# A hybrid S5 / short-conv / SwiGLU layer on one core: three pairs interleaved at the start, whole fp32 products for two block products, branch setup from step 0, smaller activation pieces, cosine product staged

## The chip, the core and the metric

One core of a Trainium2 chip runs the whole layer as one program. Its engines are TensorE (PE, matmul; PEld is its weight load), VectorE (DVE), ScalarE (ACT), GpSimd (POOL) and the DMA queues, nearly all issued from SyncE (SP). Each engine takes its instructions in the written order and waits on semaphores where an operand or a buffer is not ready. The metric is the device time of one execution in microseconds, the median over runs.

## The reference

```python
proj = jnp.einsum('bsd,dn->bsn', x, w_in) + b_in            # 1024 x 1024 -> 4096 columns
u, h, c_gate, b_gate, gate_a, gate_b = jnp.split(proj, [o1, o2, o3, o4, o5], axis=-1)
y_a = s5_ssm(u, ...)                                        # complex diagonal scan, 32 groups x 64 states
g = jax.nn.gelu(y_a)
y_a = g * jax.nn.sigmoid(jnp.einsum('bsc,ce->bse', g, glu_w) + glu_b)
y_a = jnp.einsum('bsc,cd->bsd', y_a, w_ssm_out)
z = causal_depthwise_conv(c_gate * h, conv_w)
y_b = jnp.einsum('bsc,cd->bsd', b_gate * z, w_conv_out)
merged = jax.nn.sigmoid(gate_a) * y_a + jax.nn.sigmoid(gate_b) * y_b
mix = jnp.einsum('bsd,de->bse', merged, w_o)
x = layer_norm(ALPHA * x + mix, ln1_g, ln1_b)
hid = jax.nn.silu(jnp.einsum('bsd,df->bsf', x, w_gate)) * jnp.einsum('bsd,df->bsf', x, w_up)
x = layer_norm(ALPHA * x + jnp.einsum('bsf,fd->bsd', hid, w_down), ln2_g, ln2_b)
```

Everything is float32; x is 1024 tokens by 1024 channels, the feed-forward width is 2816.

## The kernel before

**Products.** Every large matrix product is done at nearly float32 precision with three fast passes: an operand is split into a high part (`hi`, rounded to fp32r by ACT) and a low part (`lo`, the rest, by DVE), and `Entry.mm` (lines 178 to 182) adds lo·hi, hi·lo and hi·hi for each of four quarters of the contraction: 12 matmuls of 128x512. The input projection and the gate/up projection use a Strassen-like scheme over 2x2 blocks: a `Pair` is two weight tiles, and seven block products m = 1 to 7 replace eight (tables `WOP`, `XOP`). Products 3 and 4 take a plain weight block, 2 and 5 take a plain block of x and a sum of two weight blocks, 1, 6 and 7 take sums on both sides. So each of the seven x operands (`xh[m]`, `xl[m]`, 128 x 2048 elements) must be summed (m = 1, 3, 4, 6, 7) and split once at the start of a stage, and each weight operand once per product.

**One step per product.** `run` (line 310) writes the program: at step s it issues the weight sum for step s+4 (on POOL), the weight split for step s+3 (ACT and DVE), one piece of each background generator in `bg`, the 12 matmuls of step s, then the evacuations of what that product completed (`Pair.ev`). Stage A (the input projection) has 112 steps: pairs u0 and u2 interleaved, then hc0, hc1, gt0, b0, hc2, hc3, gt1, b2 and gt2 to gt7. u is the S5 input, hc and b the conv branch, gt the gates.

**Two forms of split.** `split` (line 120) writes hi to SBUF and subtracts with both operands in SBUF. `psplit` (line 131) lets ACT write hi twice, once to a PSUM staging bank `hp` and once to SBUF, and DVE subtracts with one operand in PSUM. psplit needs two staging banks, so then a pool has six matmul banks in place of eight.

**The start.** The x operands are made in halves of 1024 columns with `split` (`make_x`); of each sum one half is on DVE and one on POOL (`sum_x`), both hooked into steps 1 to 10.

**Background work.** `setup` (line 462) is some hundred short DVE instructions of 32 to 288 columns that make the S5 tables; it starts at step 12. Then `mats`, `rot` and `flow` make eight chunks of the scan: `flow` multiplies on PE into `psw`, ACT copies it to `w`, two DMAs swap its partition halves into `ws`, and DVE multiplies `psw` by the cosine table into `w`, in place over what the swap reads (line 719). psw lies in one of two PSUM slots (`sm`) that pst, pk, psw and psy of `mats` and `flow` share.

**Stage D.** The gate/up projection starts at step 168 with the pairs f0, f1, f2 interleaved over 21 steps. Its x operands (`make_x1`, line 1136) are made there in halves of 1024 columns with `split`; the PSUM pool has eight banks and no staging until step 189, so weight splits there are of the SBUF form too.

Of the kernel before, what the change touches and what calls it, by code (L numbers as in the profile page):

```python
# [47 lines left out]
def kernel(  # L48
# [121 lines left out]
    class Entry:  # L170
# [6 lines left out]

        def mm(self, ps, xh, xl, first, last):
            for k in range(4):
                PE.matmul(ps, self.lo[:, k, :], xh[:, k, :], start=first and k == 0, stop=False, skip_group_check=True)  # L180
                PE.matmul(ps, self.hi[:, k, :], xl[:, k, :], start=False, stop=False, skip_group_check=True)  # L181
                PE.matmul(ps, self.hi[:, k, :], xh[:, k, :], start=False, stop=last and k == 3, skip_group_check=True)  # L182

    class Pair:
        def __init__(self, s0, s1, nm, combos, epilogue):
# [3 lines left out]
            self.alt, self.z3, self.early, self.drops = False, None, False, {}  # L189
# [13 lines left out]
        def ev(self, m):  # L203
# [51 lines left out]
        def step(self, m):  # L255
# [19 lines left out]
            def do_mm():  # L275
# [4 lines left out]
                xh, xl = self.xc(m)  # L280
                en.mm(self.b[bi], xh, xl, first, True)
# [135 lines left out]
    def make_x(m, parts=1):  # L417
        op = XOP[m]
        h = xh[m] = xcp.tile([P, 4, 512], F32R, tag=f"xh{m}", name=f"xh{m}")
        l = xl[m] = xcp.tile([P, 4, 512], F32R, tag=f"xl{m}", name=f"xl{m}")  # L420
        if len(op) == 1:
            s = 4 // parts
            for q in range(parts):
                c = slice(s * q, s * q + s)
                split(h[:, c], l[:, c], xr[op[0]][:, c])
        else:
            for q in range(2):
                c = slice(2 * q, 2 * q + 2)
                split(h[:, c], l[:, c], xsum[m][q])

    xsum = {}

    def sum_x(m):
        op = XOP[m]
        a, b = xr[op[1]], xr[op[2]]
        xsum[m] = []
        for q in range(2):
            t = sp.tile([P, 2, 512], F32, tag="xsum", name=f"xs{m}_{q}", bufs=3)
            c = slice(2 * q, 2 * q + 2)
            tt(t, a[:, c], b[:, c], OPS[op[0]], G if q else V)  # L440
            xsum[m].append(t)

    pairs[1].alt = lambda nm: epi.tile([P, T], F32, tag="cv", name=nm, bufs=2)[:, 0:512]
    add_pairs(pairs, LEAD_A, 2)
# [16 lines left out]
    def setup():  # L461
        ramp = tb["ramp"] = stile([P, P], "ramp", "ramp")
        dss = tb["dss"] = stile([16, NG], "dss", "dss")
        mg = tb["mg"] = stile([P, 2], "mg", "mg")
        V.memset(mg[:, 0:1], MAGIC)
        V.memset(mg[:, 1:2], -MAGIC)
        nc.sync.dma_start(dss, dsk)
        nc.sync.dma_start(ramp, cst[:, P : 2 * P])
        nLre = tb["nLre"] = stile([P, NG, 9], "nLre", "nLre")
        Lim = tb["Lim"] = stile([P, NG, 9], "Lim", "Lim")  # L470
        Mre = tb["Mre"] = stile([P, NG, 8], "Mre", "Mre")
        sMim = tb["sMim"] = stile([P, NG, 8], "sMim", "sMim")
        E8 = tb["E8"] = stile([P, NG], "E8", "E8")
        ph8 = tb["ph8"] = stile([P, 2, NG], "ph8", "ph8")
        scr = [stile([P, 4 * P], t, f"scr_{t}") for t in ("w", "ws", "z", "zs")]
        used = [0] * 4

        def carve(*shape):
# [41 lines left out]
        th, hh, hl = carve(NG), carve(NG), carve(NG)  # L520
# [10 lines left out]
        V.scalar_tensor_tensor(pr[:, 3], hh, C3, pr[:, 3], ALU.mult, ALU.add)  # L531
        wrap(pr, tm)
# [6 lines left out]
        wrap(phh, th)  # L539
        add(phl, pr[:, 3], pr[:, 2])  # L540
# [1118 lines left out]
```

## Time and profile before

| | |
|---|---|
| median of three runs | 1295.02 us (1293.82 to 1295.74) |
| the profiled execution | 1294.12 us, span 1292.3 us |
| PE busy | 1207.6 us, 93% of the span |
| DVE busy | 860.5 us, 67% |
| POOL busy | 783.4 us, 61% |
| ACT busy | 737.0 us, 57% |
| DMA queue of SP | 38.2% of 16 engines, 123 GB/s to and from HBM |

The page gives PE's share over the whole span; what is left over, 85 us, is not spread evenly. Its line of 40 slices shows PE at 7 to 8 tenths in the first two slices (32 us each), at 9 nearly everywhere later, at 6 in the slice at 646 us, and at 7 to 6 in the last two. DVE and POOL show 8 or 9 tenths in just these early slices and around 646 us. So a reader looks at the start, at the stretch from 160 to 406 us with the scan's chunks, and at the start of stage D one by one.

### The profile page before, as it was taken

The numbers are of one execution on the slowest core, as the hardware profiler recorded it, in microseconds if no ns is written. First come the engines' busy times: TensorE is split into PE (matmuls) and PEld (weight loads), VectorE is DVE, ScalarE is ACT, GpSimd is POOL, SyncE is SP. The second block draws the span as 40 slices with busy tenths as digits, with TensorE's granted clock in tenths as the row PEclk, the third lists the DMA queues.
The fourth block names the chain that finished last, engine by engine and source line by source line (L and its number), as shares of the span: only waits on it lengthen the run. The fifth ranks groups of instructions, "written<-read, shape, count | busy, mean of one in ns | idle before, by whom it ended". The sixth has DMA issues, their size and how long they took to land. (4 is left out here: it accounts for less than half of the span.)

```text
span 1292.3 us, 16665 instructions
## 1 busy us (share of the span) xinstructions
PE 1207.6 (93%) x5365; PEld 981.3 (76%) x5365; DVE 860.5 (67%) x1319; ACT 737.0 (57%) x1288; POOL 783.4 (61%) x579
## 2 busy tenths in 40 slices
PE   7789899989899999999869999999999999999976
PEld 4577677777677888888757888888888887888756
DVE  6998688786676675688984444444344467667797
ACT  5645776778776252243433555555555555878841
POOL 4836878796862125123688777778778764544444
PEclk9989999999999999999989999999999999999988
DMA  5221343344446645224204423323222419845212
GB/s 198 74 94 46 103 117 97 116 153 144 141 140 223 204 139 199 79 98 147 98 33 145 165 82 114 106 91 122 107 98 98 155 66 348 296 135 171 70 54 77
DMA packets 88023, 166.07 MB, mean 129 GB/s; under 512 B 17792, under 2 KB 27008, under 8 KB 87680
## 3 DMA queue, kind: packets, MB, share of 16 engines
q1 hardware_dynamic: 87936, 165.00, 38.2%
q8 instruction: 43, 0.70, 0.2%
q14 instruction: 44, 0.36, 0.1%
HBM read 114.77 MB, written 44.83 MB: 123 GB/s over the span
## 5 line engine op out<-in xcount | busy, mean ns | idle before, releaser
L180 PE MATMUL ps_f<-x1h,wl_f 128*128 128x512 f32 x616 | 242.5, 394 | 13.1 <-DVE wl_f L115 9.5
L181 PE MATMUL ps_f<-x1l,wh_f 128*128 128x512 f32 x616 | 241.6, 392 | 2.8 <-DVE x1l L115 2.8
L182 PE MATMUL ps_f<-x1h,wh_f 128*128 128x512 f32 x616 | 241.3, 392 | 0.0
L115 DVE TENSOR_TENSOR wl_f<-t_f,hp 128x512 fp32r<-128x512 f32 x92 | 63.3, 688 | 166.0 <-ACT hp L137 166.0
L180 PEld LDWEIGHTS ps_f<-x1h,wl_f 128*128 128x128 f32 x616 | 116.7, 190 | 39.7 <-issue 8.5
L137 ACT ACTIVATE hp<-t_f 128x512 fp32r<-128x512 f32 x92 | 55.4, 602 | 148.7 <-POOL t_f L106 147.8
L181 PEld LDWEIGHTS ps_f<-x1l,wh_f 128*128 128x128 f32 x616 | 116.7, 189 | 27.7 <-DVE x1l L115 3.6
L182 PEld LDWEIGHTS ps_f<-x1h,wh_f 128*128 128x128 f32 x616 | 116.6, 189 | 24.3
L1481 PE MATMUL pe<-rBl,rAh 128*128 128x512 f32 x297 | 117.7, 396 | 8.8 <-DVE rBl L115 8.8
L106 POOL TENSOR_TENSOR tB<-B,B 128x512 f32<-128x512 f32 x55 | 71.3, 1296 | 83.1 <-DVE rBl L115 47.6
L1480 PE MATMUL pe<-rBh,rAl 128*128 128x512 f32 x297 | 117.6, 396 | 1.5 <-DVE acc L112 1.3
L1482 PE MATMUL pe<-rBh,rAh 128*128 128x512 f32 x297 | 116.9, 394 | 0.0
L180 PE MATMUL ps_gt<-xh,wl_gt 128*128 128x512 f32 x224 | 90.0, 402 | 5.4 <-ACT ea_gt L227 2.4
L182 PE MATMUL ps_gt<-xh,wh_gt 128*128 128x512 f32 x224 | 88.3, 394 | 0.0
L181 PE MATMUL ps_gt<-xl,wh_gt 128*128 128x512 f32 x224 | 87.7, 392 | 0.0
L106 POOL TENSOR_TENSOR t_f<-raw_f,raw_f 128x512 f32<-128x512 f32 x62 | 83.3, 1344 | 4.1 <-DVE wl_f L115 4.1
L1481 PEld LDWEIGHTS pe<-rBl,rAh 128*128 128x128 f32 x297 | 56.4, 190 | 23.8 <-DVE rBl L115 12.4
L1480 PEld LDWEIGHTS pe<-rBh,rAl 128*128 128x128 f32 x297 | 56.5, 190 | 14.9 <-DVE acc L112 2.1
L1482 PEld LDWEIGHTS pe<-rBh,rAh 128*128 128x128 f32 x297 | 56.5, 190 | 11.6
L106 POOL TENSOR_TENSOR t_f<-raw_f 128x512 f32<-128x512 f32 x43 | 57.2, 1340 | 10.2 <-DMA raw_f<-in_wgu 9.6
L109 POOL TENSOR_TENSOR hid<-sgf,ec_f 128x512 f32<-128x512 f32 x21 | 27.5, 1309 | 55.0 <-DVE sgf L109 31.8
L115 DVE TENSOR_TENSOR rAl<-As,hp 128x512 fp32r<-128x512 f32 x66 | 45.3, 687 | 20.7 <-ACT hp L137 14.9
(406 smaller groups left out, 3283.7 us busy)
## 6 DMA issues: line engine op xcount, KB each, us to landing
raw_f<-in_wgu SPq DMA_DIRECT2D x45, 512.0 KB, 3.9
As<-a_d SPq DMA_DIRECT2D x77, 256.0 KB, 3.5
a_d<-hs SPq DMA_DIRECT2D x55, 256.0 KB, 2.0
B<-in_wd SPq DMA_DIRECT2D x44, 256.0 KB, 5.3
raw_gt<-in_w SPq DMA_DIRECT2D x16, 512.0 KB, 4.5
s_d<-sg SPq DMA_DIRECT2D x32, 256.0 KB, 2.6
sgd<-s_d SPq DMA_DIRECT2D x16, 512.0 KB, 3.6
a_d<-hid SPq DMA_DIRECT2D x22, 256.0 KB, 2.2
```

The costliest lines, as they stand in the source:

```text
L106: eng.tensor_tensor(o, a, b, op)
L109: eng.tensor_tensor(o, a, b, ALU.mult)
L115: eng.tensor_tensor(o, a, b, ALU.subtract)
L137: S.activation(hp, raw, AF.Copy)
L180: PE.matmul(ps, self.lo[:, k, :], xh[:, k, :], start=first and k == 0, stop=False, skip_group_check=True)
L181: PE.matmul(ps, self.hi[:, k, :], xl[:, k, :], start=False, stop=False, skip_group_check=True)
L182: PE.matmul(ps, self.hi[:, k, :], xh[:, k, :], start=False, stop=last and k == 3, skip_group_check=True)
L1480: PE.matmul(ps, al[:, c], bh, start=kp == 0, stop=False)
L1481: PE.matmul(ps, ah[:, c], bl, start=False, stop=False)
L1482: PE.matmul(ps, ah[:, c], bh, start=False, stop=kp == NK - 1)
```

## The change

- The pair gt0 is drawn forward: u0, u2 and gt0 are interleaved over the first 21 steps, in the product order that stage D has (`LEAD`).
- For these three pairs, products 2 and 5 are done with four unsplit float32 matmuls (`mm_whole`) of the plain x quarter and the plain weight sum (`wsum`); x operands 2 and 5 are split last, for the pairs behind.
- `make_x` works in quarters of 512 columns, one per call, all sums on POOL, with `split` and `psplit` in turn, hooked behind the matmuls of steps 0 to 19.
- `setup` starts at step 0, cut into more pieces, with its tables in a pool of their own; five small loads go out on ACT's queue. The small PSUM pool opens at step 21, not 14.
- `flow` writes the cosine product at once into a staging tile `wc`; `z` has two buffers; the next chunk's scan waits for the rotation and not for `y`; `psy` comes one step later; `K` lies in a staging tile.
- Stage D has six banks and staging from its first step; `make_x1` works in quarters with `split` and `psplit` in turn; f2's first two banks are copied to SBUF (`kept`).

```diff
+        def mm_whole(self, ps, w, x, first, last):
+            for k in range(4):
+                PE.matmul(ps, w[:, k, :], x[:, k, :], start=first and k == 0, stop=last and k == 3, skip_group_check=True)
...
+            if self.kept:
+                for i, need in ((0, {2, 4}), (1, {5, 3})):
+                    if once(f"k{i}", need):
+                        kt = self.kept(i)
+                        S.activation(kt, self.b[i], AF.Copy)
+                        self.b[i] = kt
...
             def do_split(c=slice(0, 4)):
+                if m in self.whole:
+                    return
...
-                xh, xl = self.xc(m)
-                en.mm(self.b[bi], xh, xl, first, True)
+                if m in self.whole:
+                    en.mm_whole(self.b[bi], hold["t"], xr[XOP[m][0]], first, True)
+                else:
+                    en.mm(self.b[bi], *self.xc(m), first, True)
...
-    pairs = [mkpair(0, 1, "u0", epi_u, 0), mkpair(2, 3, "u2", epi_u, 2)]
     gp_ = [mkpair(16 + d, 24 + d, f"gt{d}", epi_g, d) for d in range(8)]
+    pairs = [mkpair(0, 1, "u0", epi_u, 0), mkpair(2, 3, "u2", epi_u, 2), gp_.pop(0)]
...
+    def make_x():
+        waiting = []
+
+        def low(h, l, k, src):
+            (psplit if k % 2 else split)(h[:, k], l[:, k], src)
+
+        for n, m in enumerate((4, 3, 1, 7, 6, 5, 2)):
+            op = XOP[m]
+            if len(op) == 3:
+                sums = xcp.tile([P, 4, 512], F32, tag=("xh2", "xl2")[n % 2], name=f"xs{m}")
+            h = xh[m] = xcp.tile([P, 4, 512], F32R, tag=f"xh{m}", name=f"xh{m}")
+            l = xl[m] = xcp.tile([P, 4, 512], F32R, tag=f"xl{m}", name=f"xl{m}")
+            for k in range(4):
+                if len(op) == 1:
+                    src = xr[op[0]][:, k]
+                else:
+                    src = sums[:, k]
+                    tt(src, xr[op[1]][:, k], xr[op[2]][:, k], OPS[op[0]], G)
+                waiting.append((h, l, k, src))
+                if len(waiting) > 2:
+                    low(*waiting.pop(0))
+                yield 1
...
+    for p in pairs[:3]:
+        p.drops = {4: 1}
+        p.whole = {2: wsum, 5: wsum}
+    add_pairs(pairs, LEAD, 3)
...
         ws = stile([P, 4, P], "ws", f"ws{cc}")
         swap(ws, w)
-        s["sin"] = True
+        c = slice(0, 127)
+        wc = stage(f"wc{cc}").rearrange("p (g k) -> p g k", g=4)
+        mul(wc[:, :, c], ps[:, :, c], s["C"])
         yield 2
-        c = slice(0, 127)
         mul(ws[:, :, c], ws[:, :, c], s["S"], G)
-        mul(w[:, :, c], ps[:, :, c], s["C"])
         yield 1
-        add(w[:, :, c], w[:, :, c], ws[:, :, c])
-        while cc and "y" not in st[cc - 1]:
+        add(w[:, :, c], wc[:, :, c], ws[:, :, c])
+        while cc and "rotated" not in st[cc - 1]:
             yield 1
-        z = stile([P, 4, P], "z", f"z{cc}")
+        z = stile([P, 4, P], "z", f"z{cc}", 2)
...
-        yield 3
+        s["rotated"] = True
+        yield 4
...
+        for q in range(4):
+            c = slice(128 * q, 128 * q + 128)
             if len(op) == 1:
                 src = blk(op[0])[:, q]
             else:
...
+                tt(src, blk(op[1])[:, q], blk(op[2])[:, q], OPS[op[0]], V if m == 7 and q % 2 else G)
+            yield lambda c=c, src=src, q=q: (psplit if q % 2 else split)(h[:, :, c], l[:, :, c], src)
...
+    fps[2].kept = lambda i: cst_["zp"].tile([P, 512], F32, tag=f"keep{i}", name=f"keep{i}")
...
     def begin_d0():
+        flush()
+        psum_open("psD", 6, True)
...
+    xg = make_x()
+    for n, cnt in enumerate((2, 2, 2, 1, 2, 1, 2, 1, 2, 1, 2, 1, 2, 2, 1, 2, 1, 1, 1, 1)):
+        steps[n].mid.append(lambda cnt=cnt: [next(xg, None) for _ in range(cnt)])
+    start(setup())
...
-    steps[12].pre.append(begin_ssm)
-    steps[14].pre.append(small_psum)
+    steps[21].pre.append(lambda: (flush(), small_psum()))
```

**DVE, first stage.** Before, around the split of x operands 1 and 4 (`xl` is a low part of x, `xs` a sum of x, `wl` a low part of a weight, `hp` a staging bank in PSUM):

```order
L115 TENSOR_TENSOR xl_212<-xs_1_186,xh_211 128x1024
L115 TENSOR_TENSOR wl_u_1_218<-t_u_1_188,hp_219 128x512
L106 TENSOR_TENSOR xs_0_239<-xr_109,xr_90 128x1024
L115 TENSOR_TENSOR wl_u_4_244<-raw_u_1_89,hp_245 128x512
L115 TENSOR_TENSOR xl_265<-xs_0_239,xh_264 128x1024
L115 TENSOR_TENSOR xl_265<-xs_1_241,xh_264 128x1024
L115 TENSOR_TENSOR wl_u_4_271<-raw_u_1_100,hp_272 128x512
```

After, around x operands 3 and 1 (`scr` is the scratch tile of `setup`):

```order
L115 TENSOR_TENSOR xl_208<-xs_206,hp_299 128x512
L115 TENSOR_TENSOR wl_u_3_307<-raw_u_0_110,hp_308 128x512
L545 SCALAR_TENSOR_TENSOR scr<-scr 128x32 x3
L118 TENSOR_SCALAR scr<-scr 128x32
L547 SCALAR_TENSOR_TENSOR scr<-scr 128x32
L115 TENSOR_TENSOR xl_273<-xs_271,xh_272 128x512
L115 TENSOR_TENSOR xl_273<-xs_271,hp_326 128x512
L106 TENSOR_TENSOR eb_u_330<-ps_u_0_149,ea_u_159 128x512
```

The sums of x have left DVE, the low parts are half as long and every second one reads PSUM, and the short instructions of `setup` stand between them.

**DVE, the second scan chunk of stage A.** Before, the cosine product stands close ahead of the sum that uses it:

```order
L109 TENSOR_TENSOR w_1351<-psw_1346,ctab_1087 128x4x127
L112 TENSOR_TENSOR eb_b_1296<-ps_b_2_1315,eb_b_1296 128x512
L115 TENSOR_TENSOR wl_hc_1_1427<-t_hc_1_1403,hp_1428 128x512
L112 TENSOR_TENSOR w_1351<-w_1351,ws_1353 128x4x127
L726 MEMSET zs_1441 128x4
```

After, it goes to a tile of its own (`wc`) and eight instructions lie between:

```order
L109 TENSOR_TENSOR wc_1203<-psw_1193,ctab_932 128x4x127
L112 TENSOR_TENSOR eb_hc_1070<-ps_hc_2_1099,eb_hc_1070 128x512
L115 TENSOR_TENSOR wl_gt_1_1222<-t_gt_1_1178,hp_1223 128x512
L115 TENSOR_TENSOR cp_1189<-cp_1189,ct_1190 128x576
L378 SCALAR_TENSOR_TENSOR zE_1245<-ps_hc_0_1016,b1s,hs_1146 128x512
L112 TENSOR_TENSOR ec_hc_1112<-ps_hc_3_1231,ec_hc_1112 128x512
L115 TENSOR_TENSOR wl_gt_4_1251<-raw_gt_1_1008,hp_1252 128x512
L378 SCALAR_TENSOR_TENSOR zE_1245<-ec_hc_1112,b1s,hs_1146 128x512
L115 TENSOR_TENSOR wl_gt_3_1278<-raw_gt_0_1032,hp_1279 128x512
L112 TENSOR_TENSOR w_1198<-wc_1203,ws_1200 128x4x127
```

The product is issued two steps earlier and no longer writes what the swap's DMAs read.

## Rows read from the trace of the kernel before

**Rows 1.** Stretches: length, busy (instructions) of PE, PEld, DVE, ACT, POOL, clock, DMA

```profile
12.60:60.90 48.30, 36.79 (x140) 26.21 (x139) 43.36 (x34) 32.09 (x49) 40.62 (x18) 1.00 0.32 108
160.00:200.00 40.00, 36.80 (x175) 30.01 (x176) 33.78 (x49) 26.62 (x48) 30.46 (x23) 0.92 0.38 114
200.00:406.00 206.00, 190.04 (x927) 155.18 (x925) 146.88 (x207) 158.31 (x266) 148.84 (x108) 1.00 0.46 140
627.00:676.20 49.20, 35.93 (x140) 27.56 (x139) 46.67 (x31) 19.49 (x29) 41.98 (x20) 0.92 0.13 50
```

**Rows 2.** Timeline of DVE and POOL, first 75 us: start, length, instruction

```profile
27.90 1.21 DVE L106 TENSOR_TENSOR xs<-xr,xr 128x1024 f32<-128x1024 f32 x1
...
30.24 2.38 POOL L106 TENSOR_TENSOR xs<-xr,xr 128x1024 f32<-128x1024 f32 x1
...
44.88 3.49 POOL L106 TENSOR_TENSOR xs<-xr,xr 128x1024 f32<-128x1024 f32 x1
...
46.02 0.68 DVE L115 TENSOR_TENSOR wl_u<-t_u,hp 128x512 fp32r<-128x512 f32 x1
...
57.36 1.28 POOL L106 TENSOR_TENSOR t_hc<-raw_hc 128x512 f32<-128x512 f32 x1
...
69.00 0.19 DVE L499 SCALAR_TENSOR_TENSOR scr_z<-scr_z 128x32 f32<-128x32 f32 x1
...
73.17 1.32 POOL L112 TENSOR_TENSOR ea_hc<-ea_hc,eb_hc 128x512 f32<-128x512 f32 x1 [7.52 <-ACT eb_hc L230]
...
73.37 1.17 DVE L501 TENSOR_SCALAR scr_zs<-scr_zs 128x32 f32<-128x32 f32 x1
```

**Rows 3.** Groups in 12.6 to 60.9 us: count, busy us, mean ns, idle before

```profile
L106 POOL TENSOR_TENSOR xs<-xr,xr 128x1024 f32<-128x1024 f32 x5 | 15.1, 3010 | 0.0
...
L115 DVE TENSOR_TENSOR xl<-xs,xh 128x1024 fp32r<-128x1024 f32 x10 | 21.3, 2134 | 2.7 <-ACT xh L121 2.5
L106 DVE TENSOR_TENSOR xs<-xr,xr 128x1024 f32<-128x1024 f32 x5 | 9.1, 1824 | 0.0
...
L115 DVE TENSOR_TENSOR xl<-xr,xh 128x1024 fp32r<-128x1024 f32 x2 | 3.5, 1770 | 0.8 <-ACT xh L121 0.8
```

**Rows 4.** Timeline of PE: first matmuls of products 15, 16 and 22

```profile
66.75 0.39 PE L180 MATMUL ps_hc<-xh,wl_hc 128*128 128x512 f32 x1
...
69.49 0.39 PE L180 MATMUL ps_hc<-xh,wl_hc 128*128 128x512 f32 x1
...
89.97 0.80 PE L180 MATMUL ps_hc<-xh,wl_hc 128*128 128x512 f32 x1 [3.83 <-DVE ec_hc L112]
```

**Rows 5.** Timeline of PE: unsplit float32 matmuls, two instructions to each

```profile
259.83 0.63 PE L642 MATMUL pst<-ident,bst 128*128 128x128 f32 x4 [2.09 <-ACT gy L768]
...
289.63 1.03 PE L648 MATMUL pk<-cp,bst 128*16 128x128 f32 x8 [1.48 <-DVE w L109]
```

**Rows 6.** PE's waits in 160 to 406 us, and the timeline around the longest

```profile
PE pk L648 <- DVE w L109: 11.9, 4, 5.5
PE psy L741 <- DVE z L115: 3.9, 3, 1.6
...
158.29 1.68 DVE L115 TENSOR_TENSOR cp<-cp,ct 128x576 f32<-128x576 f32 x1
...
163.20 1.86 PE L648 MATMUL pk<-cp,bst 128*16 128x128 f32 x8 [5.54 <-DVE w L109]
```

**Rows 7.** Groups of POOL and DVE in 627.0 to 676.2 us

```profile
L106 POOL TENSOR_TENSOR x1s<-M 128x1024 f32<-128x1024 f32 x6 | 19.2, 3207 | 4.7 <-DVE x1l L115 4.7
...
L115 DVE TENSOR_TENSOR wl_f<-t_f,wh_f 128x512 fp32r<-128x512 f32 x9 | 14.4, 1604 | 0.0
L115 DVE TENSOR_TENSOR x1l<-x1s,x1h 128x1024 fp32r<-128x1024 f32 x8 | 14.0, 1763 | 0.0
L115 DVE TENSOR_TENSOR x1l<-M,x1h 128x1024 fp32r<-128x1024 f32 x2 | 4.9, 2492 | 1.0 <-ACT x1h L121 1.0
L106 DVE TENSOR_TENSOR x1s<-M 128x1024 f32<-128x1024 f32 x2 | 4.5, 2292 | 0.0
```

More of the change, by code (lines that the diff above doesn't have):

```diff
@@ L262, in do_add @@
                 if len(op) == 3:
-                    if "t" not in hold:
+                    if "t" not in hold and m in self.whole:
+                        hold["t"] = self.whole[m]()
+                    elif "t" not in hold:
                         hold["t"] = wring.tile([P, 4, P], F32, tag="tmp", name=f"t_{self.nm}_{m}", bufs=2)
@@ L314, in run @@
             if s + 4 < len(steps) and steps[s + 4].add:
-                steps[s + 4].add(eng=V if steps[s + 4].addv else G)
+                steps[s + 4].add()
             if s + 3 < len(steps) and steps[s + 3].split:
@@ L431 @@
[L431 to L444, printed above, removed]
+    def make_x():
[18 more added lines that the diff above has]
+                yield 1
+        for w in waiting:
+            low(*w)
+            yield 1
@@ new lines, in load_f, with wsum @@
+    def load_f(p, i):
+        p.raw[i] = epi.tile([P, T], F32, tag="cv", name=f"xz{i}", bufs=2).rearrange("p (k q) -> p k q", k=KT)
+        nc.sync.dma_start(p.raw[i], p.src[i])
+    wsums = []
+    def wsum():
+        n = len(wsums)
+        if n in (0, 4):
+            wsums.append(xcp.tile([P, 4, 4, P], F32, tag=("xh5", "xl5")[n // 4], name=f"ws{n}"))
+        else:
+            wsums.append(wsums[n - 1])
+        return wsums[n][:, n % 4]
+    pairs[1].alt = stage
+    pairs[2].early = True
@@ L472, in setup, with carve @@
[L472 to L478, printed above, removed]
+        scr = xst.tile([P, 1216], F32, tag="scr", name="scr")
+        used = [96]
+        def carve(*shape, at=None):
             n = int(np.prod(shape))
-            i = min(i for i in range(4) if used[i] + n <= 4 * P)
-            t = scr[i][:, used[i] : used[i] + n]
-            used[i] += n
+            o = used[0] if at is None else at
+            if at is None:
+                used[0] += n
+            t = scr[:, o : o + n]
@@ L592, in setup @@
         ts(nLre, nLre, sgn[:, 0:1], -1.0, ALU.mult, ALU.mult)
+        while next(xg, None):
+            yield 1
+        close(xst_cm)
+        open_ssm()
         Tt = tb["T"] = []
@@ L1232, in x1_rest @@
     def x1_rest():
+        waiting = []
         for m in (3, 1, 7, 6):
[L1234 to L1239 removed]
+            for f in make_x1(m):
+                waiting.append(f)
+                if len(waiting) > 2:
+                    waiting.pop(0)()
+                yield
+        for f in waiting:
+            f()
+            yield
     x1g = x1_rest()
[L1241 removed]
+    for n, cnt in ((4, 2), (5, 2), (6, 2), (7, 2), (8, 1), (9, 2), (10, 1), (11, 2), (12, 2), (13, 2), (14, 1)):
         steps[n_d + n].mid.append(lambda cnt=cnt: [next(x1g, None) for _ in range(cnt)])
@@ L1324 @@
     nc.sync.dma_start(cws, convw)
-    x2h = xh[2] = xcp.tile([P, 4, 512], F32R, tag="xh2", name="xh2")
-    x2l = xl[2] = xcp.tile([P, 4, 512], F32R, tag="xl2", name="xl2")
     for q in range(2):
-        c = slice(2 * q, 2 * q + 2)
-        steps[0].add(c, V)
-        steps[0].split(c)
-        for k in (2 * q, 2 * q + 1):
-            split(x2h[:, k], x2l[:, k], x00[:, k])
+        steps[0].add(slice(2 * q, 2 * q + 2), V)
+    steps[0].split()
     steps[1].add(eng=V)
```

145 lines of the change are left out of this document (57 added, 88 removed).

## The prediction, written before the changed kernel was run

> **What bounds the kernel now.** I read the page first: PE is busy 93% of the span, so no other engine bounds the whole, and only PE's 85 us of idle time and a low clock can be given back. Then I asked stretch by stretch what PE waits for. A step at full pace takes 69.49 − 66.75 = 2.74 us, 12 matmuls of 0.2285 us [rows 4]; the seven products 15 to 21 keep that pace, and one wait of 3.83 us stands behind them, just before product 22 [rows 4].
>
> In the start, 12.6 to 60.9 us, PE is idle 48.3 − 36.8 = 11.5 us, and DVE (43.4) and POOL (40.6) are both nearly full, ACT (32.1) is not [rows 1]. The mean durations there are too long: a sum of x takes POOL 3.0 us and DVE 1.8, a low part of x takes DVE 2.1 [rows 3], while the shortest of the same shapes take 2.38 and 1.21 [rows 2]. One place shows why: a DVE instruction of 32 columns takes 0.19 us alone and 1.17 when it begins 0.2 us into a POOL instruction that ends at 74.49 [rows 2]. The two exclude each other when DVE has both operands in SBUF; low parts of weights, which read one operand in PSUM (`hp`), keep 0.68 even there (46.02, inside a POOL sum) [rows 2]. So I add POOL's work and DVE's SBUF-only work at their undisturbed lengths. In 12.6 to 60.9: POOL 13 x 1.28 + 5 x 2.38 = 28.5, DVE 17 x 1.21 = 20.6, in all 49.1 in 48.3 us, a ratio of 0.98. That sum, not PE, sets the start. In 627.0 to 676.2, where stage D makes its operands and PE is idle 13.3 us [rows 1], POOL has 6 x 2.38 + 12 x 1.28 = 29.6, DVE 12 x 1.21 + 13 x 0.68 = 23.4: 53.0 in 49.2, a ratio of 0.93. There even the low parts of weights are slow, 1.6 us [rows 7], since they are of the SBUF form.
>
> Between 160 and 406 us PE loses 3.2 + 16.0 us [rows 1], of which 11.9 are four waits of `pk` for `w` (the cosine product and its sum on DVE) and 3.9 three waits of `psy` for `z` [rows 6]. The granted clock is 0.92 in 160 to 200 and in 627 to 676 [rows 1]; by that the matmuls there take 36.8 x 0.08 = 2.9 us longer, twice.
>
> **The start.** Removed: five halves of x sums on DVE and twelve low parts of 1024 columns, 17 x 1.21 on the shared path. Added up to the operands of product 22: POOL 39 instructions of 512 columns at 1.28 = 49.9; DVE SBUF-only 14 quarters of low parts at about 0.68 (an estimate from 1.21 for twice the width) = 9.5; `setup` 62 short ones at 0.19 = 11.8, and 14 wider ones between 0.19 and 0.68, 5.7 by width. In all 76.9, by 0.98 75.4 us. The first stretch starts at 12.7 as before, so product 22 would start at 88, where it now starts at 89.97 [rows 4], because today `setup` is paid behind step 14 and ends in the wait of 3.83. But DVE also has 44 instructions with a PSUM operand, 30 us. The sum supposes that all of them run beside POOL. DVE is in order: its own work is 57 us, and each of the 39 POOL instructions can hold it once for at most 1.28. If half of that is lost, DVE needs 57 + 25 = 82 and product 22 starts at 95. I take 92, between them: +2.
>
> PE itself would allow 12.7 + 21 x 2.74 + the surplus of the unsplit products. No row has one; the small fp32 matmuls bound it: eight instructions of 128 columns took 1.03, four took 0.63 [rows 5], so 0.10 each or, with the fixed part, 0.13. A 512-column product of one quarter is eight such, 0.80 to 1.03, a step 3.2 to 4.1, against 2.74; six steps cost 2.8 to 8.3 us. I take 5.5, the middle: PE's floor for product 22 is 76. With 92 taken, the 5.5 lie in PE's idle time; in the second rival they count. They also spare six low parts of weights on DVE and the ACT copies for them. Reloads of three weights, 1.5 MB more on SP's queue, fall where DMA is 0.32 busy [rows 1]: nothing; if that cover were gone the weight sums would wait for them.
>
> **The scan's chunks.** `w` no longer waits for the swap's reads and the cosine product is issued two steps earlier. In the longest wait PE stood 5.54 us, from 157.66 to 163.20, but `pk` needs `cp` too, and that ended at 158.29 + 1.68 = 159.97 [rows 6]. So 2.3 of 5.54 would stay, 42%; of 11.9 I take 58% away: −6.9. Bounds: 0, if `cp` or the swap is last everywhere, and −11.9. `psy` a step later and `z` in two buffers: between 0 and −3.9, I take −3, since the longest of the three waits is 1.6, less than a step. If PE stands less, the clock may not fall; of 2.9 I take half, −1.5. Against it: `wc` and `K` share the four staging tiles, and `K` keeps its tile until eight DMAs have landed; the evacuations behind it on DVE wait for a tile, and PE for those. Neither the wait nor such an eight-fold hold is in this trace; it costs 0 to one step per chunk (8 x 2.74 = 22, if every chunk stops a step, the upper end); the pauses of the kind now in the trace (rest of PE's waits, about 5 us in all) make me take +2. Sum −9.
>
> **Stage D.** POOL's sums go from 6 x 2.38 to 14 x 1.28 (+3.6), `t_f` moves from DVE to POOL (+0.6), low parts of x1 on the shared path from 10 x 1.21 to 10 x 0.69 (−5.2), sums on DVE from 2 x 1.21 to 2 x 0.69 (−1.0), and 12 low parts of weights leave it because they read PSUM (−8.2). −10.2 by 0.93 is −9.4, less than PE's 13.3 us of idle time. Half of the 2.9 of clock: −1.5. Sum −11. ACT has psplit's second write more, some 24 x 0.6 = 14 us over a stretch in which it is busy 19.5 of 49.2 [rows 1]: nothing, up to +5 if six banks in place of eight make PE wait for evacuations queued behind it. Bounds −16 to +3.
>
> **Sum.** +2 − 9 − 11 = −18 from the profiled execution's 1294.1: 1276 us. That execution is 0.9 us under the median, 0.07%, so nothing is added.
>
> **The rivals.** *First, slower:* DVE stands behind POOL in the start. Sixty-two short instructions, dependent on one another, are strewn over 39 POOL instructions, each a chance to be held as at 73.37 [rows 2]; low parts of weights and evacuations stand behind them in order. If every POOL instruction holds DVE for its 1.28, DVE needs 57 + 49.9 = 107 us, by 0.98 105: product 22 starts at 118, +28, and with −20 elsewhere the time is 1302. It decides from a start of product 22 at 110. For it: 1.17 for 0.19; against it: in the stretch now, 12 us of PSUM-operand work lay wholly beside POOL (49.1 of SBUF work filled 48.3).
>
> The Trainium skill, "SBUF — State Buffer", section "SBUF: two separate sides", states that the pair of ports shared by GpSimd and VectorE is an exclusive lock that whoever starts first holds for the whole instruction. The 1.17 for 0.19 agrees with that; it speaks against this change, since by it sums moved from DVE to POOL give the shared path back nothing and each short instruction can wait for a whole POOL one, which is this rival; the sum above, without such waits, would come to 1272.
>
> *Second, a shorter start:* DVE works in the gaps, POOL's instructions need not be as early as I count them, and PE's floor holds: product 22 at 76, −14, and the time is 1260. For it: ACT and the DMA have room; against it: the shared sum of 75 us in place of 63.
>
> *Third, waits that only move:* `pk` finds `cp`, the swap or a staging tile late, and the chunks give −1 rather than −9: 1284; or stage D gives only −2, because PE waits for banks: 1285; both, 1293. For it: `cp` ends 2.3 us into the wait [rows 6]; against: POOL and DVE really lose 10 us of shared work in D.
>
> **How the numbers follow.** The forecast 0.50, with 1264 to 1288 as its own range (±4 for the start, ±6 for the chunks, ±6 for D). Second rival 0.13. Third 0.19, of which 0.03 ends near 1293. First rival 0.18, of which 0.12 is full (over 1297) and the rest a half version that ends between 1283 and 1296. About 0.2%, 2.6 us, is what can be told from no change: 1292.4 to 1297.6 is the same. Faster: 0.50 + 0.13 + 0.16 + 0.04 = 0.83; same 0.03 + 0.02 = 0.05; slower 0.12. The range 1254 to 1298 leaves out the first rival's full form for the most part and the second's lower tail, 0.15 together.
>
> **What would show it.** Right: product 22 starts near 92 us; PE's waits of `pk` fall to about 5 us in all; PE's idle time at the start of stage D falls from 13.3 us to 2 to 6, with low parts of weights at 0.68. Wrong: product 22 after 110, with many short `setup` instructions over 1 us and POOL at 2 us or more; `pk` waiting on `cp` or DVE on a staging tile; PE in stage D waiting for an evacuation. The unsplit products are right if a step of four takes 3.2 to 4.1 us.

## The result, and the profile after

The changed kernel takes 1288.08 us (median of four runs, 1286.10 to 1289.52), the kernel before 1295.05 on the same chip: a ratio of 0.9943, 95% interval [0.9928, 0.9958]. It is faster by 7.0 us, where 18 were forecast.

| | before | after |
|---|---|---|
| span of the profiled execution | 1292.3 us | 1284.9 us |
| PE busy | 1207.6 | 1214.3 |
| DVE busy | 860.5 | 849.7 |
| POOL busy | 783.4 | 786.3 |
| ACT busy | 737.0 | 758.4 |

The stretches of [rows 1], in the changed kernel (length, then busy time of PE, PEld, DVE, ACT, POOL, granted clock, DMA share):

```profile
12.60:60.90 48.30, 41.39 (x129) 25.64 (x128) 45.43 (x74) 28.14 (x51) 37.04 (x29) 0.93 0.42 146
160.00:200.00 40.00, 40.00 (x202) 33.26 (x201) 33.09 (x50) 27.65 (x48) 31.03 (x23) 1.00 0.36 111
200.00:406.00 206.00, 194.84 (x925) 156.84 (x924) 150.84 (x210) 157.52 (x266) 150.14 (x108) 0.99 0.46 140
627.00:676.20 49.20, 43.11 (x164) 33.63 (x163) 36.72 (x47) 36.08 (x68) 42.04 (x31) 0.86 0.13 50
```

PE's idle time falls in each of them, from 13.3 to 6.1 us in the last. But equal windows do not hold equal work, and in the start the clock is lower. The honest measure is when the same product starts, read off PE's timeline. Product 22 is the first behind the new interleaved start, 31 the first behind `setup` in both kernels, 112 the last of stage A, 113 the first and 145 the 33rd of stage D:

| profiled execution, us | product 22 | 22 to 31 | 31 to 112 | 112 to 113 | 113 to 145 | rest | end |
|---|---|---|---|---|---|---|---|
| before | 89.97 | 30.13 | 284.42 | 208.93 | 110.33 | 568.5 | 1292.3 |
| after | 106.49 | 26.45 | 272.61 | 207.57 | 102.14 | 569.6 | 1284.9 |
| difference | +16.5 | −3.7 | −11.8 | −1.4 | −8.2 | +1.1 | −7.4 |

So the start costs 16.5 us at product 22 and still 12.85 at product 31. From product 31 to the end of the table's last stretch 21.4 us are gained, a little more than the 20 that were forecast for the chunks and stage D. PE's waits in 5 to 130 us of the changed kernel (total, times, longest):

```profile
PE ps_gt L183 <- ACT ec_gt L237: 9.4, 1, 9.4
PE ps_u L183 <- DVE scr L118: 5.4, 1, 5.4
...
PE ps_gt L183 <- DVE wl_gt L115: 5.0, 1, 5.0
PE ps_u L183 <- ACT z_u L237: 2.0, 1, 2.0
PE ps_u L184 <- DVE xl L115: 1.9, 1, 1.9
...
PE ps_hc L183 <- DVE ec_gt L112: 0.8, 1, 0.8
```

The 5.0 us are the low part of a weight that stands in DVE's order behind `setup`. Timelines of DVE and POOL just before it (start, length, instruction):

```profile
43.80 1.28 POOL L112 TENSOR_TENSOR z_u<-z_u 128x512 f32<-128x512 f32 x1
43.86 1.29 DVE L556 COPY scr<-scr 128x32 f32<-128x32 f32 x1
...
45.04 3.91 DVE L109 TENSOR_TENSOR scr<-scr 128x32 f32<-128x32 f32 x3
45.05 1.29 POOL L106 TENSOR_TENSOR t_u<-raw_u,raw_u 128x512 f32<-128x512 f32 x1
...
48.98 1.13 DVE L560 COPY E<-scr 128x32 f32<-128x32 f32 x1
50.03 0.68 DVE L115 TENSOR_TENSOR xl<-xs,xh 128x512 fp32r<-128x512 f32 x1
50.63 0.68 DVE L106 TENSOR_TENSOR z_u<-ps_u,z_u 128x512 f32<-128x512 f32 x1
51.23 0.67 DVE L115 TENSOR_TENSOR wl_gt<-xz,hp 128x512 fp32r<-128x512 f32 x1
```

Instructions of 32 columns take 1.13 to 1.3 us each, as the one at 73.37 did in [rows 2]: POOL is at its additions of 1.28 us. All 76 of `setup` before 98 us take 46.4 us. The 9.4 us stand at the end of that queue (timeline of DVE, ACT and PE):

```profile
94.51 0.68 DVE L112 TENSOR_TENSOR z_u<-ps_u,z_u 128x512 f32<-128x512 f32 x1
95.37 0.72 ACT L358 ACTIVATE us<-z_u,b1s 128x512 f32<-128x512 f32 x1 [0.94 <-DMA u_d<-us]
96.51 0.58 ACT L237 ACTIVATE ec_gt<-ps_gt 128x512 f32<-128x512 f32 x1
...
97.14 0.80 PE L183 MATMUL ps_gt<-xh,wl_gt 128*128 128x512 f32 x1 [9.37 <-ACT ec_gt L237]
...
106.49 0.50 PE L183 MATMUL ps_hc<-xh,wl_hc 128*128 128x512 f32 x1 [0.78 <-DVE ec_gt L112]
```

Product 19 ended at 87.8. ACT's copy `ec_gt`, which takes its result out, stands behind `us` activations that need DVE's sums (`z_u`), and DVE is late. Products 19 and 20 are m = 1 and m = 7 of gt0; they write the same bank (`BANK_OF`) and stand next to each other at the end of `LEAD`, so 20 cannot begin before 19 has been copied out.

Behind the start the waits of [rows 6] are gone. PE's waits in 133 to 406 us:

```profile
PE ps_gt L183 <- ACT ea_gt L231: 3.1, 1, 3.1
PE ps_gt L183 <- DVE wl_gt L115: 1.5, 2, 1.3
PE pk L695 <- DVE cp L115: 1.3, 2, 1.0
PE ps_b L183 <- ACT ea_b L231: 1.1, 1, 1.1
...
PE psy L788 <- ACT bp L691: 0.5, 1, 0.5
```

`pk` waited 11.9 us for `w`, now 1.3 for `cp`; `psy` 3.9 us, now 0.5. In stage D the groups that answer to [rows 7], in 627.0 to 676.2 us:

```profile
L106 POOL TENSOR_TENSOR x1s<-M 128x512 f32<-128x512 f32 x14 | 20.2, 1464 | 3.9 <-ACT wh_f L138 2.5 <-DVE x1l L115 1.4
...
L115 DVE TENSOR_TENSOR x1l<-x1s,x1h 128x512 fp32r<-128x512 f32 x8 | 10.9, 1358 | 1.5 <-ACT x1h L121 1.5
...
L115 DVE TENSOR_TENSOR wl_f<-t_f,hp 128x512 fp32r<-128x512 f32 x11 | 7.5, 679 | 1.4 <-ACT hp L137 1.2
...
L115 DVE TENSOR_TENSOR x1l<-x1s,hp 128x512 fp32r<-128x512 f32 x8 | 5.4, 676 | 0.0
```

The low parts with an operand in PSUM take 0.68 us; those with both in SBUF are still stretched to 1.36. Over equal work, from product 113 to 145, PE's waits fall from 15.8 us to 6.9. The longest group of before, and the largest one that is new in the changed kernel:

```profile
PE ps_f L180 <- DVE wl_f L115: 9.5, 3, 6.5
...
PE ps_f L183 <- ACT keep L246: 1.6, 1, 1.6
```

### The profile page after: what moved, and what is told of

Read it like the earlier page. It is cut to its first block, busy times and chain, and to the rows that moved or that the text cites. A ratio compares the mean times of both kernels' runs of the same rounds, so it can differ in the third digit from the quotient of the medians.

```text
span 1284.9 us, 16758 instructions
## 1 busy us (share of the span) xinstructions
PE 1214.3 (95%) x5341; PEld 979.1 (76%) x5341; DVE 849.7 (66%) x1328; ACT 758.4 (59%) x1346; POOL 786.3 (61%) x603
## 5 line engine op out<-in xcount | busy, mean ns | idle before, releaser
L115 DVE TENSOR_TENSOR wl_f<-t_f,hp 128x512 fp32r<-128x512 f32 x107 | 73.5, 687 | 168.5 <-ACT hp L137 168.3
L137 ACT ACTIVATE hp<-t_f 128x512 fp32r<-128x512 f32 x107 | 64.4, 602 | 174.5 <-POOL t_f L106 168.1
L184 PEld LDWEIGHTS ps_f<-x1l,wh_f 128*128 128x128 f32 x616 | 117.0, 190 | 25.1 <-DVE x1l L115 1.0
L183 PEld LDWEIGHTS ps_gt<-xh,wl_gt 128*128 128x128 f32 x216 | 42.0, 195 | 32.8 <-ACT ec_gt L237 10.3
L138 ACT ACTIVATE wh_f<-t_f 128x512 fp32r<-128x512 f32 x107 | 66.0, 617 | 0.1
```

The lines of the kernel that those rows point to most:

```text
L115: eng.tensor_tensor(o, a, b, ALU.subtract)
L137: S.activation(hp, raw, AF.Copy)
L138: S.activation(hi, raw, AF.Copy)
```

## The experiments

Each is timed against the kernel before on its own chip, where that took 1293.9 to 1295.2 us; the ratios allow for this, the bare times do not. Times are medians. The stretches are those of the table above, each from one profiled execution; that lies within 1.5 us of the median but for run 4 (4.9 below it) and run 5 (2.8 above).

| | time, us | ratio to before | product 22 | 22 to 31 | 31 to 112 | 112 to 113 | 113 to 145 |
|---|---|---|---|---|---|---|---|
| changed kernel | 1288.08 | 0.9943 [0.9928, 0.9958] | 106.49 | 26.45 | 272.61 | 207.57 | 102.14 |
| 1 `setup` from step 12 | 1306.58 | 1.0086 [1.0071, 1.0102] | 104.33 | 30.57 | 283.70 | 215.06 | 101.97 |
| 2 `setup` from step 21 | 1293.74 | 0.9992 [0.9982, 1.0003] | 88.08 | 42.89 | 281.67 | 207.81 | 101.95 |
| 3 x sums on DVE | 1285.91 | 0.9927 [0.9910, 0.9944] | 102.60 | 26.44 | 275.38 | 206.75 | 102.12 |
| 4 before + flow + D | 1294.89 | 0.9994 [0.9982, 1.0006] | 89.28 | 30.16 | 280.50 | 216.60 | 103.06 |
| 5 evacuations first | 1286.63 | 0.9950 [0.9930, 0.9969] | 104.80 | 26.45 | 272.72 | 208.00 | 102.00 |
| 6 `setup` paused | 1289.62 | 0.9962 [0.9947, 0.9976] | 97.25 | 36.11 | 273.40 | 209.50 | 102.11 |
| 7 one step later | 1294.44 | 1.0002 [0.9992, 1.0012] | 106.85 | 25.21 | 280.35 | 207.47 | 102.08 |
| 8 old flow | 1300.31 | 1.0054 [1.0038, 1.0070] | 105.66 | 26.44 | 278.69 | 215.15 | 102.03 |
| 9 as 4, `setup` ends at 24 | 1280.62 | 0.9881 [0.9867, 0.9896] | 93.29 | 33.50 | 270.93 | 207.46 | 105.55 |
| 10 as 9, at 23 | 1289.32 | 0.9952 [0.9935, 0.9968] | 92.59 | 33.08 | 273.85 | 215.23 | 104.95 |
| 11 stage D alone | 1286.93 | 0.9935 [0.9920, 0.9950] | 89.18 | 30.19 | 284.75 | 210.75 | 102.30 |
| 12 as 3 and 5 | 1283.00 | 0.9904 [0.9889, 0.9918] | 102.86 | 26.46 | 273.39 | 208.08 | 102.02 |

### What holds the start

**Run 1**, `setup` from step 12, two pieces a step:

```diff
-    start(setup())
+    steps[12].pre.append(lambda: start(several(setup(), 2)))
```

> The changed kernel, but `setup` starts at step 12, two of its pieces per step, so it ends at step 22 (24 in the changed kernel). Theory A (in the start DVE is held by POOL: the 76 `setup` instructions took 46.4 us before 98 us, 0.61 us each, and weight splits and evacuations stand behind them): behind most of the x sums the same instructions take 20 to 30 us, product 22 starts at 86 to 96 us in place of 106.5, and the time is 1270 to 1280 us. Theory B (the third pair: three pairs' evacuations on ACT and six banks, `setup` only a bystander): product 22 stays at 103 us or later, the time at 1285 to 1291.

Measured: 1306.58 us, worse than either theory allowed. The instructions of `setup` did get shorter (65 of them 22.3 us up to product 20, where 76 took 46.4), and product 19 started at 76.6 in place of 84.9. But DVE, half idle up to 50 us, was now 37.5 of 42.3 us busy behind it, and product 20 waited 11.2 us for the same copy `ec_gt`. Theory A has the right price of the held instructions, but the lower price did not free product 22, since the same work was now crowded into the second half of the start. Most of the loss lies later, in the chunks (+11.1) and at 112 to 113 (+7.5), which no theory spoke of: `setup` ends two steps earlier, and runs 7 to 10 show what such a shift does.

**Run 2**, `setup` from step 21, five pieces a step:

```diff
-    start(setup())
+    steps[21].pre.append(lambda: start(several(setup(), 5)))
```

> The changed kernel, but `setup` starts at step 21, five pieces per step, and ends at step 25: none of it lies in the first 21 products. Theory A: DVE has 38 us of other work before product 22, and PE's own floor decides, product 22 at 76 to 82 us; then `setup` crowds steps 21 to 25 and costs up to 10 us there; the time is 1266 to 1278 us. Theory B: the wait of 9.4 us before product 20 and the one before product 22 stay, product 22 at 98 us or later, the time 1285 or more, since `setup` then costs again behind it.

Measured: product 22 at 88.08, 18.4 us earlier. Theory B is out: the third pair without `setup` has a wait of 3.9 before product 20, not 9.4. But PE's floor of 76 is not reached, and behind product 22 everything is paid back: 42.89 us for nine products in place of 26.45. Among PE's waits in 5 to 132 us are

```profile
PE ps_hc L183 <- DVE ec_hc L112: 5.3, 1, 5.3
...
PE ps_gt L183 <- ACT ec_gt L237: 3.9, 1, 3.9
...
PE ps_hc L183 <- DVE wl_hc L115: 2.8, 1, 2.8
...
PE ps_hc L183 <- DVE scr L118: 1.9, 1, 1.9
```

The same `setup`, undisturbed by x sums, takes DVE 27.6 us (95 instructions), against 55.4 in the changed kernel up to product 31; but set densely it keeps weights and evacuations waiting. Product 31 starts at 130.97, 2 us earlier than in the changed kernel. The time is longer all the same, by the 9.1 us from product 31 to 112: `setup` ends one step later here, and each chunk stands one step later, as in run 7.

**Run 3**, all sums of x on DVE:

```diff
-                    tt(src, xr[op[1]][:, k], xr[op[2]][:, k], OPS[op[0]], G)
+                    tt(src, xr[op[1]][:, k], xr[op[2]][:, k], OPS[op[0]], V)
```

> The changed kernel, but all 20 quarter sums of x are on DVE in place of POOL. Theory A: DVE gains 20 x 0.68 = 13.6 us of work, but POOL loses 25.1 us in which it can hold DVE, `setup` instructions fall below 0.4 us on the mean, product 22 starts at 92 to 106 us and the time is 1274 to 1288. Theory C (DVE is simply full; the holds come from the weight sums and stay): product 22 moves back by 8 to 14 us, to 114 to 120, the time is 1295 to 1302.

Measured: 1285.91 us, product 22 at 102.60. DVE was given 20 instructions more and ended earlier: `setup` up to product 20 took 32.2 us in place of 46.4. Theory C asked for a product 22 at 114 or later; it is out. The held instructions, at 0.41 us on the mean, came down nearly as theory A has it (below 0.4).

**Run 5**, in the first 21 steps evacuations ahead of epilogues and x pieces:

```diff
-            flush()
-            for f in steps[s].mid + steps[s].after:
-                f()
+            todo = []
+            if s < 21:
+                todo, later[:] = later[:], []
+                for f in steps[s].after:
+                    f()
+            else:
+                flush()
+            for f in todo + steps[s].mid + (steps[s].after if s >= 21 else []):
+                f()
```

> The changed kernel, but in the first 21 steps the evacuations of a step are issued ahead of the deferred epilogues (`us`) and the x pieces. Theory H (product 20 waits 9.4 us because ACT's copy `ec_gt`, which frees its bank, stands in ACT's order behind `us` activations that wait for DVE's sums): that wait falls under 4 us, product 22 starts at 97 to 102 us, when the low part of x operand 2 is done, and the time is 1280 to 1285. Theory K (DVE is full up to 98 us, so only the name of the wait changes): product 22 at 104 us or later, 1286 to 1290.

Measured: product 20 waits 7.4 us for `ec_gt` in place of 9.4, product 22 starts 1.7 us earlier, the time is 1286.63, by its ratio no faster than the changed kernel. Theory K: ACT's order is the last link and gives 2 us; in the 7.4 us that stay DVE is busy 96% and ACT 88%, and what share each has in them was not separated. With run 3 on top of it (**run 12**, below) the wait stays 7.45.

**Run 6**, run 5 with `setup` paused from step 13 to 21, the rest three pieces a step:

```diff
-    start(setup())
+    def paced(g):
+        for k, _ in enumerate(g):
+            if k < 12:
+                yield 1
+            elif k == 12:
+                yield 10
+            elif k % 3 == 0:
+                yield 1
...
+    start(paced(setup()))
```

> As the run before, and `setup` pauses from step 13 to 21: 13 of its 24 pieces in steps 0 to 12, the others three per step from step 22, its end again at step 24. Theory A (what DVE does in the start sets product 22): product 22 at 88 to 95 us, the eleven pieces then cost 3 to 8 us, product 31 starts at 118 to 126 (132.95 in the changed kernel), the time is 1273 to 1282. Rival (the work of `setup` is paid one to one wherever it stands): product 31 at 129 to 134, the time 1284 to 1290.

Measured: product 22 at 97.25, then 36.11 us to product 31, which starts at 133.4, as in the changed kernel and 2.1 later than in run 5. The rival is right: where `setup` stands in the start moves the wait, not product 31 by more than 2 us.

**Run 12**, the edits of runs 3 and 5 together:

```diff
+                for f in steps[s].after:
...
-                    tt(src, xr[op[1]][:, k], xr[op[2]][:, k], OPS[op[0]], G)
+                    tt(src, xr[op[1]][:, k], xr[op[2]][:, k], OPS[op[0]], V)
```

> The changed kernel with both edits of two earlier runs: x sums on DVE (product 22 at 102.6 in place of 106.5), and in the first 21 steps the evacuations ahead of epilogues and x pieces (104.8). Theory A (DVE's work up to product 20 sets the start): DVE has the same work as in the first of them, product 22 at 100 to 104 us, the time 1283 to 1287. Theory H (ACT's order keeps the banks): product 22 at 94 to 99, the time 1278 to 1282.

Measured: 1283.00 us, product 22 at 102.86: theory A. The start is not better than in run 3; the time is at its bound.

### What the later stretches are worth, and why

**Run 4**, the kernel before with the edits of `flow`, K and stage D, its start as it was:

```diff
+        wc = stage(f"wc{cc}").rearrange("p (g k) -> p g k", g=4)
+        mul(wc[:, :, c], ps[:, :, c], s["C"])
...
+        while cc and "rotated" not in st[cc - 1]:
...
     def begin_d0():
+        flush()
+        psum_open("psD", 6, True)
```

> The kernel before with only the edits of `flow` (staging tile for the cosine product, two z, the next scan waits for the rotation, psy one step later, K staged) and of stage D (six banks, quarters with split and psplit in turn, two banks copied out). Theory A: these edits gave what was gained, whatever the start does: stage D -8, the chunks -10 to -16 between product 22 and the end of stage A, so 1271 to 1277 us, faster than both kernels. Theory G (the chunks gained because the start paid `setup` early, so that the stretch behind product 22 had less to do): the chunks give -0 to -5, and the time is 1282 to 1287.

Measured: 1294.89 us, no gain. In the profiled execution, which was the fastest of ten (1290.0 to 1296.7), stage D gave its share (103.06), the chunks only 3.9 us from product 31 to 112, and 112 to 113 took 7.7 more; what the slower executions lose beyond that is not traced. Neither theory foresaw the loss at 112 to 113. Two things show in the trace. The waits for `w` have moved to `cp`, as the third rival of the prediction had it (PE's waits in 133 to 410 us):

```profile
PE pk L654 <- DVE cp L115: 5.7, 4, 2.5
PE ps_b L179 <- ACT ea_b L227: 4.3, 1, 4.3
```

And the new `flow` makes the chain of chunks longer. On PE's timeline it runs from the first `pst`, behind product 34, to the last `psy`, behind 112, the last of stage A; in the kernel before it runs from 34 to 109, in the changed kernel from 29 to 108.

**Run 7**, the changed kernel with one empty step behind `setup`:

```diff
         while next(xg, None):
             yield 1
+        yield 1
```

> The changed kernel with one empty step behind `setup`, so that each chunk's work stands one step later against the products. Theory P (the position of the chunks' steps against the seven products of a pair sets their waits): product 22 at 106 to 107 as before, from product 31 to 112 277 to 285 us in place of 272.6, the time 1292 to 1300. Theory Q (position does not matter, the setup in the start costs the second kernel its stretch): 271 to 275, the time 1287 to 1290.

Measured: product 22 as before, 280.35 us from 31 to 112 (+7.7), 1294.44 us: the whole gain is gone. Theory P. PE's waits in 133 to 410 us show what took it:

```profile
PE ps_gt L183 <- ACT ea_gt L231: 7.4, 3, 3.4
PE ps_gt L183 <- DVE ec_hc L112: 3.5, 1, 3.5
PE ps_hc L183 <- ACT ec_hc L237: 2.0, 1, 2.0
```

No wait of `pk` is among them. They are waits of products for a bank that ACT (`ea_gt`, `ec_hc`) or DVE (`ec_hc`) has to empty; for `ea_gt` three, 7.4 us in all, where the changed kernel has one of 3.1.

**Run 8**, the changed kernel with the edits of `flow` and K undone:

```diff
-        mul(wc[:, :, c], ps[:, :, c], s["C"])
+        mul(w[:, :, c], ps[:, :, c], s["C"])
...
-        while cc and "rotated" not in st[cc - 1]:
+        while cc and "y" not in st[cc - 1]:
```

> The changed kernel with the edits of `flow` and of K undone (cosine product in place, one z, the wait for y, psy three steps on). Theory F (these edits took away the waits of `pk` for `w`): those waits come back with 9 to 12 us, from product 31 to 112 it takes 282 to 288 us in place of 272.6, the time is 1297 to 1303. Theory G (an early `setup` gave it): no more than 277 us, the time 1287 to 1292.

Measured: `pk` waits for `w` again, 8.2 us in three waits; 31 to 112 takes 6.1 us more, less than theory F's 9 to 15, and 112 to 113 takes 7.6 more, which brings the time to 1300.31, in the range that it named but in part for another reason.

**Run 9**, run 4 with shorter pauses in `setup`, so that it ends at step 24 and each chunk stands at the step of the changed kernel; **run 10** the same, ending at 23:

```diff
-        start(setup())
+        start(hasten(setup(), 0.76))
```

`hasten` multiplies the pauses between the pieces by the number, which is 0.70 in run 10.

> The kernel before with the edits of `flow` and of stage D, and `setup` still from step 12 but with shorter pauses, so that it ends at step 24 and every chunk stands at the steps of the changed kernel. Theory P (position of the chunks): the start keeps nearly the time of before, product 31 at 121 to 126 us; from product 31 to 112 272 to 276, to product 113 207 to 209, stage D 102 to 103; the time is 1274 to 1281, faster than both kernels. Rival (a faster `setup` behind step 12 is paid one to one, or the chunks need the changed kernel's order of pairs): product 31 at 128 or later or the stretch to 112 over 280, the time 1284 to 1292.

> As the run before, but `setup` ends at step 23, so each chunk's work stands one step earlier. Theory P: the stretch from product 31 to 112 differs by 5 us or more from the run before; the time by as much, 1278 to 1290. Rival (only the end of the chain counts): the same within 3 us.

Measured: run 9 takes 1280.62 us, 0.9881 of before [0.9867, 0.9896], the fastest of all, 7.5 us under the changed kernel. Product 31 starts at 126.8, a little late, 31 to 112 takes 270.93, and stage D keeps only 4.8 of its 8.2: PE waits 3.9 us for `keep` and 4.1 for `wl_f` there, where the changed kernel has 1.6 and 1.8. Run 10 is 8.7 us slower, by 2.9 from 31 to 112 and by 7.8 at 112 to 113. Theory P had said 5 or more for the first; there its rival's "within 3 us" held. Over all runs the stretch from 31 to 112 goes with the step: six kernels whose chunks stand on the changed kernel's steps (it, and runs 3, 5, 6, 9 and 12) have 270.9 to 275.4 us, one step later 280.4 and 281.7 (runs 7 and 2), one earlier 273.9 (run 10), two earlier 283.7 (run 1). The 7.8 are a matter of order on ACT. Run 10, where stage B begins:

```profile
397.56 0.62 ACT L121 ACTIVATE wh_so<-raw_so 128x512 fp32r<-128x512 f32 x1
...
405.05 1.40 ACT L771 ACTIVATE gl<-gy 128x512 f32<-128x512 f32 x2 [6.87 <-DMA gy<-y_d]
406.36 0.71 ACT L397 ACTIVATE sg<-eb_gt,b1s 128x512 f32<-128x512 f32 x1
406.98 0.61 ACT L121 ACTIVATE vh<-vr_z 128x512 fp32r<-128x512 f32 x1
407.64 0.79 PE L179 MATMUL pso<-vh,wl_so 128*128 128x512 f32 x1 [5.20 <-ACT vh L121]
```

Run 9 at the same place:

```profile
398.65 0.72 ACT L397 ACTIVATE sg<-eb_gt,b1s 128x512 f32<-128x512 f32 x1 [2.27 <-DVE eb_gt L112]
399.35 0.64 ACT L121 ACTIVATE vh<-vr_z 128x512 fp32r<-128x512 f32 x1
...
404.34 1.31 ACT L771 ACTIVATE gl<-gy 128x512 f32<-128x512 f32 x2
```

`gl` is the last chunk's gelu and waits for `y` to come back from memory; `vh` is what stage B's first product needs. With the chain one step earlier, `gl` is written ahead of `vh`, and PE waits through its transfer. In runs 1 and 8 `gl` stands ahead of `vh` too, with waits of 6.1 and 5.3 us; in run 4, whose chain ends last, `vh` waits 4.5 us for its own load. PE's wait for `vh` is 5.2 to 5.9 us in these four. They show 215 to 217 us from 112 to 113, all others 207 to 211.

**Run 11**, the kernel before with stage D's edits alone:

```diff
     def begin_d0():
+        flush()
+        psum_open("psD", 6, True)
...
+            yield lambda c=c, src=src, q=q: (psplit if q % 2 else split)(h[:, :, c], l[:, :, c], src)
```

> The kernel before with the edits of stage D alone. All theories: the stretch from product 113 to 145 takes 102 to 103 us in place of 110.33, all else as before, the time 1286 to 1288. If something of it is given back behind stage D: 1289 or more.

Measured: 1286.93 us, stage D 8.0 us shorter, as expected and to the end. This part alone gives as much as the whole change.

## Why the prediction was wrong, point by point

**The direction was right, the size was not: −7.0 against −18.** By its terms, in the profiled execution: the start +16.5 at product 22 (+2 said); the chunks, from product 22 to 113, −16.9 (−9 said), of which −3.7 lie before product 31, where the kernel before still pays for `setup`; stage D −8.2 (−11 said); the rest +1.1 (nothing said).

**The start is the step that failed**, in "DVE needs 57 + 25 = 82 and product 22 starts at 95. I take 92". DVE's sum was good: from 12.6 to 97.1 us it had 46.4 of `setup` (17.5 by the prediction's own lengths, so 28.9 held), 25.1 with a PSUM operand and 13.2 of low parts, 84.7. Two things failed. The 92 was taken below the 95 of that sum, and DVE's work ended at 97.1, 5.1 us behind 92. And product 22 does not start at DVE's end; product 20 does, since its bank is freed by a copy that hangs on the same queue of work (97.14), and then come two products at the lower clock, 5.29 and 4.06 us, the other 9.4 of the 14.5 us by which 92 was missed. Run 2 has a wait of 3.9 us at product 20 even without `setup`. The first rival's mechanism held, at six tenths of its price (16.5 of 28), and 106.5 is 3.5 us short of its point of decision; that the whole still became faster is due to the later stretches.

Behind that lies a worse choice of mark. `setup` was moved from behind product 15 to ahead of product 22, so a comparison at 22 counts a cost that the kernel before pays later. At product 31 the start costs 12.85, and PE's two timelines account for it: 4.1 for the unsplit products at full pace, 5.5 of waits (29.6 against 24.1, all of PE's waits up to there), 1.8 of matmuls slower than full pace (15.5 against 13.7) and 1.4 for the first chunk's small matmuls, which stand behind product 31 in the kernel before. Run 9, whose `setup` also ends at step 24, reaches product 31 at 126.79: against that the new start loses 6.2. Up to there DVE's other work with both operands in SBUF, mostly for x operands, fell from 36.2 to 16.3 us, as forecast, and `setup` rose from 31.2 to 55.4: what was saved on operands was lost on short instructions held by POOL. Runs 2 and 6 show that moving `setup` inside the new start or behind it changes product 31 by no more than about 2 us; run 3 shows that fewer POOL sums do, by 3.9. How much the third pair costs without the unsplit products was not tried.

The Trainium skill, "SBUF — State Buffer", section "SBUF: two separate sides", speaks of an exclusive lock that is held for a whole instruction; the 1.13 to 1.3 us of 32 columns agree. It spoke against the change and was given 0.18 as a rival.

**The unsplit products** were taken at 5.5 us for six, between 2.8 and 8.3. One product takes 3.43, so 0.69 more, 4.1 in all. Timeline of two of them, 16 instructions:

```profile
30.79 7.03 PE L179 MATMUL ps_u<-xr,ws 128*128 128x512 f32 x16
```

They were taken to lie in PE's idle time. No run separates them from the rest of the start, so nothing shows that they did.

**The chunks:** the steps named were right (`pk`'s waits for `w` gone, `cp` next at 1.3), the size was not, and the reason is one that the prediction did not have. In the changed kernel the `flow` edits are worth 13.7 us (run 8: 6.1 before product 112 and 7.6 behind it). In the old place they gain 3.9 and lose 7.7 (run 4). One step later in the new place, 7.7 of the gain is lost (run 7). So no price of the edit by itself exists: the end of `setup` at step 24 decides on which steps of a pair each chunk falls, and whether `gl` or `vh` comes first. The text on the change says that `setup` starts at step 0; what that does to the chunks' steps, and that the new `flow` lengthens the chain, was not worked out. That step 24 was a good one is luck, as far as the prediction goes. The staging ring, charged with +2, shows no wait among PE's.

**Stage D:** the mechanism held (low parts of weights 0.68, from 1.6), and PE's idle time fell from 13.3 to 6.1, just over the 2 to 6 that were named. The clock term has the wrong sign: 0.86 in place of 0.92. One new wait came in, of the kind that the third rival named, 1.6 for a bank's copy (`keep`); the one for `eb_f` was there before, 2.7, and is 2.0.

**The rivals:** the second (floor of 76) did not come. The kernels with the new start and all of `setup` in it have product 22 at 102.6 to 106.9, and even without `setup` it is 88.1. The third came in part: in stage D by the one wait for `keep`, and for the chunks in full in run 4, where `pk` waits 5.7 us for `cp`, but not in the changed kernel.

## What to carry to other kernels

Judge a moved block of work at a mark that lies behind it in both versions, and sum an in-order engine's queue up to the first thing that releases the bottleneck, not up to the stage's end. Short instructions on an engine that shares its access with another are not priced at their own length: here 76 took 0.61 us each on the mean beside POOL's x sums, those of 32 columns up to 1.3, and 95 took 0.29 without them. Where background work runs in step with a loop of products, one step of shift was worth 6 to 9 us here, as much as the change itself: try the neighbouring steps before pricing an edit, and time each part alone: stage D's part by itself gave all that the whole change did, and the old start with the new chunks, put on the right step, twice that.

## What the runs showed of the hardware that was not expected

The cost of a wait does not end with it. After the 5.01 us before product 12 the changed kernel's matmuls start 0.43 us apart, at a granted clock of 0.51 (52.0 to 55.4 us), the 1.2 GHz level; from 55.48 us on they start 0.23 apart again, at 1.00 (55.5 to 60.0 us):

```profile
52.05 0.77 PE L183 MATMUL ps_gt<-xh,wl_gt 128*128 128x512 f32 x1 [5.01 <-DVE wl_gt L115]
52.61 0.63 PE L184 MATMUL ps_gt<-xl,wh_gt 128*128 128x512 f32 x1
53.04 0.63 PE L185 MATMUL ps_gt<-xh,wh_gt 128*128 128x512 f32 x1
...
55.48 0.40 PE L185 MATMUL ps_gt<-xh,wh_gt 128*128 128x512 f32 x1
55.72 0.39 PE L183 MATMUL ps_gt<-xh,wl_gt 128*128 128x512 f32 x1
```

That product took 4.41 us in place of 2.74, so the wait cost 6.7 us, not 5.0. The three later waits of the start (5.4, 2.0 and 9.4 us) are also followed by matmuls 0.43 apart. The kernel before waits in short pieces. The granted clock of that stretch is 1.00 in [rows 1], and only behind the last two pieces, 1.5 and 1.9 us, do eight matmuls start 0.41 to 0.43 apart, at 0.50 (60.8 to 64.2 us). Its waits, and two lines of PE's timeline:

```profile
PE ps_u L181 <- DVE xl L115: 9.9, 10, 1.9
...
59.77 0.51 PE L181 MATMUL ps_u<-xl,wh_u 128*128 128x512 f32 x1 [1.86 <-DVE xl L115]
...
60.82 0.62 PE L182 MATMUL ps_u<-xh,wh_u 128*128 128x512 f32 x1
```
